# A decoder layer's MLP: additions of finished banks ahead of weight preparation, MLP buffers in other places, and a narrow first matmul in the second up unit

## The chip, the cores and the metric

The kernel runs on one core of a Trainium2 chip. The metric is the device time of one execution in microseconds (us). Five engines work beside each other, each on its own queue in order: TensorE (PE, with its weight loads PEld), VectorE (DVE), ScalarE (ACT), GpSimd (POOL) and SyncE (SP), which here issues nearly all DMA transfers. Matmuls accumulate in eight banks of PSUM; everything else lies in SBUF.

## The reference

One layer of a hybrid decoder: 256 tokens (T), model width 2048, MLP width 8192, all in float32.

```
h = rmsnorm(x, g_mix) @ w_in          # one projection for all head groups
y_ssd = ...                           # Mamba-2 heads, gated norm
y_att = ...                           # sparse attention with an indexer
x = x + concatenate([y_ssd, y_att]) @ w_out
u = rmsnorm(x, g_mlp) @ w_up
return x + square(relu(u)) @ w_down
```

The change touches the last two lines alone, the MLP.

## The kernel before, in words

**Precision.** TensorE multiplies in a reduced float32 type (fp32r). Every operand is therefore split into a rounded part "hi" and a remainder "lo", and a product is three matmuls: hi·hi, lo·hi and hi·lo (`three`, L199, L201, L202). The weights are split on the chip while they stream: `operands` issues the load (L151, tile `raw`, in the MLP `rawm`), ScalarE casts hi (L154) and VectorE forms lo = raw − hi (L155), both into one tile `w2`, in the MLP `w2m`. There are three `rawm` and three `w2m` buffers. This weight preparation runs under `tc.high_priority(offset=HP)`, HP = 600.

**Order.** TensorE's order is the order of the program. On the other engines a scheduler orders instructions by what they depend on and by priority; a higher offset puts an instruction earlier. Each engine then takes its queue strictly in the order written.

**Up.** The MLP width is worked in three parts h, of 10, 11 and 11 units of 256 columns (`PARTS`). `up(h)` computes a part: for each unit, `product_w` takes two weight tiles (c = 0, 1), with 16 steps each of a 512-column and a 256-column matmul (L240), 64 matmuls in all. ScalarE and VectorE make r from the banks (copy L847, add, square of relu) and split it into `uh` and `ul` (L862, L863). The very first unit is multiplied before the MLP's pools are open, with weights from the earlier pool `wts`.

**Down.** `down(h)` multiplies a part's units with the second weight matrix in two halves j of 1024 output columns. Each half goes over the part's units, here called pairs g. A pair is done in one of two ways. `plain` has 8 products (24 matmuls) from one `w2m`. `seven` has 7 products (21 matmuls) by a scheme of Strassen's kind; its weights are sums t of blocks (VectorE, L885 and L888; lo L891) in a `w2m`, and three blocks in a tile `wb` (L883, lo L890). Of `t` and `wb` there is one buffer each. A table `SEVEN` marks the pairs 1, 3, 5 and 7 (in two halves 9 too) as `seven`, so a half begins plain, seven, plain, seven.

**Banks.** The eight banks are four of tag "mid" and four of tag "acc". A half accumulates in four banks `outs` (`acc[b][c]`) of one tag; its seven-products use four more, `ps7`, of the other tag. So the first `seven` pair of the second half takes the four banks in which the first half accumulated. They come free when VectorE has done `add` (L910): xr += acc · rs4, 128x512 each, four of them. `ps7` is copied into a tile `m` (ScalarE, L937), combined by VectorE (L938, L939, L940) and added to xr by two additions of 1024 columns (also L910). In the last part the first half's four finished blocks of xr are then written out (L912).

**Memory.** `mid_stack.close()` gives the pools `wts` (57824 to 116448, in bytes of a partition) and `mid` (116448 to 213984) back before the MLP's pool opens. The MLP's tiles are then laid into the same addresses, and the first writer of a new tile waits for the last reader of the old ones there.

**Cutting.** `interrupted(kind)` tells whether something else was multiplied since the last product of that kind. If so, `product_w` splits its first matmul into 32 (FIRST_W) and 480 columns.

Of the kernel before, what the change touches and what calls it, by code (L numbers as in the profile page):

```python
# [9 lines left out]
F32 = mybir.dt.float32  # L10
F32R = mybir.dt.float32r
# [5 lines left out]
P = 128  # L17
D = 2048
T = 256
NB = T // P  # L20
# [7 lines left out]
HP = 600  # L28
# [3 lines left out]
WIDE_B = 3  # L32
# [3 lines left out]
SPARE = 64  # L36
# [11 lines left out]
PARTS = (0, 10, 21, 32)  # L48
# [5 lines left out]
E, G, P1, F, M6 = range(5)  # L54
# [34 lines left out]
def hymba_kernel(ctx: ExitStack, tc: tile.TileContext, xn, xt, w_in, w_out, w_up, w_down, vcol, vrow, out):  # L89
    nc = tc.nc  # L90
# [42 lines left out]
    mlp_pool = []  # L133

    def operands(src, n, load=None, shift=0, parts=2):

        pitch = (n + 63) // 64 * 64
        with tc.high_priority(offset=HP):
            if mlp_pool:
                raw = mlp_pool[0].tile([P, parts, pitch], F32, name="rawm", bufs=WIDE_R)  # L140
                both = mlp_pool[0].tile([P, 2 * parts * pitch + SPARE], F32R, name="w2m", bufs=WIDE_B)
            else:
                raw = wts.tile([P, parts, pitch], F32, name="raw", tag="raw", bufs=RB)
                both = wts.tile([P, 2 * parts * pitch + SPARE], F32R, name="w2", tag="w2", bufs=WB)
            hi, lo = (both[:, shift + i * parts * pitch:shift + (i + 1) * parts * pitch]
                      .rearrange("p (k c) -> p k c", k=parts)[:, :, :n] for i in range(2))
            src = src.rearrange("p (k c) -> p k c", k=parts)
            step = parts if load is None else 1
            for i in range(0, parts, step):
                s = slice(i, i + step)  # L150
                nc.sync.dma_start(raw[:, s, :n], src[:, s])  # L151
                if load is not None:
                    load()
                nc.scalar.copy(hi[:, s], raw[:, s, :n])  # L154
                nc.vector.tensor_tensor(lo[:, s], raw[:, s, :n], hi[:, s].bitcast(F32), op=OP.subtract)  # L155
        return hi, lo

    other = []
# [64 lines left out]
        other.append("narrow")  # L223
        return acc

    def product_w(src, right, tag="acc"):

        acc = [accumulator(tag), accumulator(tag)]
        n = KT if mlp_pool else 8
        for at in range(0, KT, n):  # L230
            for c, out in enumerate(acc):
                hi, lo = operands(src[c][:, at * P:(at + n) * P], P, shift=SHIFT_W, parts=n)
                for k in range(n):
                    x = right(at + k)
                    todo = [(hi, 0, 2 * T), (lo, 0, T)]

                    if interrupted("wide"):
                        todo[:1] = [(hi, 0, FIRST_W), (hi, FIRST_W, 2 * T - FIRST_W)]
                    for j, (w, fr, m) in enumerate(todo):
                        nc.tensor.matmul(walk(out[:, fr:fr + m]), w[:, k], walk(x[:, fr:fr + m]),  # L240
                                         start=(at + k + j == 0), stop=(at + k == KT - 1 and j == len(todo) - 1),
                                         skip_group_check=True)
                    if k % 4 == 3:
                        step()
        other.append("wide")
        return acc
# [50 lines left out]
    for name, cols in IN_BLOCKS:  # L297
        n = sum(b - a for a, b in cols)
# [440 lines left out]
    xr = []  # L739
# [72 lines left out]
    xr, box, ss2, squares = run()  # L812
# [6 lines left out]
    first = product_w(w_up[0], x2)  # L819
# [13 lines left out]
    mid_stack.close()  # L833


    mlp = ctx.enter_context(tc.tile_pool(name="mlp", bufs=1))
    mlp_pool.append(mlp)

    def up(h, tag):

        u = []
        for g in range(PARTS[h + 1] - PARTS[h]):
            n = (4, 8, 7)[sum(g in marked for marked in SEVEN[h])]
            full = mlp.tile([P, 8, P], F32, name="r")
            r = full[:, :4].rearrange("p (c b) t -> p c (b t)", c=2)
            for c, acc in enumerate(first if h + g == 0 else product_w(w_up[PARTS[h] + g], x2, tag)):
                nc.scalar.copy(r[:, c], acc[:, T:])  # L847
                nc.vector.tensor_tensor(r[:, c], r[:, c], acc[:, :T], op=OP.add)
            nc.vector.scalar_tensor_tensor(r, r, 0.0, r, op0=OP.max, op1=OP.mult)
            if n > 4:  # L850

                s3 = full[:, S3[n]]
                nc.vector.tensor_tensor(s3, full[:, A11], full[:, A21], op=OP.subtract)
                nc.vector.tensor_tensor(full[:, S2], full[:, A22], s3, op=OP.add)
                nc.vector.tensor_tensor(full[:, S1::2], full[:, A11:A22:2], full[:, S2, None].to_broadcast([P, 2, P]),
                                        op=OP.subtract)
            if h == 0 and g == 3:
                junk = mlp.tile([P, 5, 512], F32, name="m")
                row_factors([junk[:, b] for b in range(NB)])
            uh = mlp.tile([P, n, P], F32R, name="uh", tag=f"uh{g}", bufs=1)  # L860
            ul = mlp.tile([P, n, P], F32R, name="ul", tag=f"ul{g}", bufs=1)
            nc.scalar.copy(uh, full[:, :n])  # L862
            nc.vector.tensor_tensor(ul, full[:, :n], uh.bitcast(F32), op=OP.subtract)  # L863
            u.append((uh, ul))
        return u
# [7 lines left out]
    def seven(src):  # L873

        with tc.high_priority(offset=HP):
            raw = mlp.tile([P, 4, 512], F32, name="rawm", bufs=WIDE_R)
            nc.sync.dma_start(raw, src.rearrange("p (k c) -> p k c", k=4))
            t = mlp.tile([P, 4, 512], F32, name="t")
            wb = mlp.tile([P, 2 * 3 * 512 + SPARE], F32R, name="wb")
            wt = mlp.tile([P, 2 * 4 * 512 + SPARE], F32R, name="w2m", bufs=WIDE_B)  # L880
            (hb, lb), (ht, lt) = [[w[:, SHIFT + i * n * 512:SHIFT + (i + 1) * n * 512]
                                   .rearrange("p (k c) -> p k c", k=n) for i in range(2)] for w, n in ((wb, 3), (wt, 4))]
            nc.scalar.copy(hb, raw[:, 1:])  # L883

            nc.vector.tensor_tensor(t[:, :2], raw[:, 1::2], raw[:, :1].to_broadcast([P, 2, 512]), op=OP.add)  # L885
            nc.scalar.copy(ht[:, :2], t[:, :2])  # L886
            for i in range(2, 4):
                nc.vector.tensor_tensor(t[:, i], t[:, 2 * (i - 2)], raw[:, 5 - i], op=OP.add)  # L888
            nc.scalar.copy(ht[:, 2:], t[:, 2:])  # L889
            nc.vector.tensor_tensor(lb, raw[:, 1:], hb.bitcast(F32), op=OP.subtract)  # L890
            nc.vector.tensor_tensor(lt, t, ht.bitcast(F32), op=OP.subtract)  # L891
        return [(hb[:, i], lb[:, i]) for i in range(3)] + [(ht[:, i], lt[:, i]) for i in range(4)]

    def down(h, u, tags):
        pairs = len(u)
        for j in range(2):
            marked = SEVEN[h][j]
            end = h == 2 and j == 1
            outs = [accumulator(tags[j]) for _ in range(4)]
            acc = [outs[:2], outs[2:]]  # L900
# [7 lines left out]
            def add(b, c, src, store=False):  # L908
                c = slice(1024 * j + c.start, 1024 * j + c.stop)
                nc.vector.scalar_tensor_tensor(xr[:, b, c], src, rs4[:, b:b + 1], xr[:, b, c], op0=OP.mult, op1=OP.add)  # L910
                if store:
                    nc.sync.dma_start(out[b * P:(b + 1) * P, c], xr[:, b, c])  # L912

            half = [slice(0, 512), slice(512, 1024)]
            ps7 = None
            kept = []
            for g in range(pairs):
                w = (seven if g in marked else plain)(w_down[j, PARTS[h] + g])
                if g in marked:
# [12 lines left out]
                    go(acc[1][0], u[g], A22, t4, False)  # L932
                    if done:

                        m = mlp.tile([P, 5, 512], F32, name="m", bufs=1)
                        for i, p in ((P1, p1), (F, p5), (E, p7), (M6, p6)):
                            nc.scalar.copy(m[:, i], p)  # L937
                        nc.vector.tensor_tensor(m[:, M6], m[:, P1], m[:, M6], op=OP.subtract)  # L938
                        nc.vector.tensor_tensor(m[:, E], m[:, M6], m[:, E], op=OP.add)  # L939
                        nc.vector.tensor_tensor(m[:, G:F + 1:2], m[:, F, None].to_broadcast([P, 2, 512]), m[:, E::4],  # L940
                                                op=OP.subtract)
                        for b, i in ((0, P1), (1, E)):
                            add(b, slice(0, 1024), m[:, i:i + 2].rearrange("p k c -> p (k c)"))
                elif end and g >= pairs - 2:
                    kept.append((u[g], w))
                else:
# [2 lines left out]
                            for b in range(NB):  # L949
                                go(acc[b][c], u[g], 2 * k + b, w[k][c], g + k == 0, g == pairs - 1 and k == 1)  # L950
            if not end:
                for c in range(2):
                    for b in range(NB):
                        add(b, half[c], acc[b][c], h == 2)
                other.append("down")
                continue

# [5 lines left out]
            c = slice(0, 256)  # L963
# [4 lines left out]
            c = slice(256, 512)  # L968
# [75 lines left out]
```

## Time and profile before

| what | value |
|---|---|
| times of three runs | 1102.87, 1095.23, 1102.21 us; median 1102.21 |
| profiled execution | 1099.45 us |
| its span, first to last instruction | 1097.6 us |
| mean granted TensorE clock | 0.984 |
| TensorE busy | 1063.8 us, 97% |
| VectorE busy | 811.6 us, 74% |
| ScalarE busy | 560.0 us, 51% |
| DMA | 207.35 MB, mean 189 GB/s |
| first load of the MLP's own pool | 396.18 us |

The profile is of one execution. A row of the timeline gives the start, the busy time, the engine and line, the operation with out<-in, and in brackets how long the engine had been idle before and what ended that. A row of a window gives its length, the busy time of PE, PEld, DVE, ACT and POOL with the count of instructions, then the granted clock of TensorE (1.00 is full speed), the DMA engines' busy share and GB/s. Ends of matmuls are modelled: neighbouring rows overlap, and the distance from start to start tells the rate.

### The profile page before, as it was taken

Reading aid. Unit: us, or ns where it says so; the run is one execution under the profiler, and the core shown is the slowest. Engines: PE = TensorE matmul, PEld = TensorE weight load, DVE = VectorE, ACT = ScalarE, POOL = GpSimd, SP = SyncE. Lnnn points to the kernel's source line nnn. Section 1 sums busy time; section 2 is a strip of 40 time slices with the busy share of each in tenths; the row PEclk is TensorE's granted clock in tenths of the full one; section 3 lists DMA queues with packets and bytes.
Section 4 is the critical chain, followed back from the end, with each engine's and each line's share of the span. In section 5 each row is a group of like instructions: output and inputs, shape, how many; then the busy total and the mean of one; then the engine's idle time right before and its main releaser. Section 6 shows DMA issues by size and latency. Waiting matters only on the chain.

```text
span 1097.6 us, 14923 instructions
## 1 busy us (share of the span) xinstructions
PE 1063.8 (97%) x5937; PEld 938.4 (85%) x5937; DVE 811.6 (74%) x1014; ACT 560.0 (51%) x675; POOL 25.2 (2%) x30
## 2 busy tenths in 40 slices
PE   9999999999999969999979999999889999999798
PEld 7999999888888858888868888888778888888687
DVE  6777998687665555679886767699877666698965
ACT  7755455566654434455635344455535444455452
POOL 0020000121000000000000000000000000000000
PEclk9999999999999989999989999999989999999899
DMA  9865447543465445555645555546546555545552
GB/s 327 265 212 173 156 118 230 170 150 125 155 238 191 135 186 197 192 195 191 229 153 192 195 193 213 203 177 213 214 135 222 192 192 192 192 178 205 201 182 77
DMA packets 45461, 207.35 MB, mean 189 GB/s; under 512 B 5072, under 2 KB 9424, under 8 KB 29264
## 3 DMA queue, kind: packets, MB, share of 16 engines
q1 hardware_dynamic: 45248, 206.35, 54.2%
q8 instruction: 47, 0.77, 0.3%
q14 instruction: 22, 0.18, 0.0%
q10 hardware_dynamic: 144, 0.05, 0.0%
HBM read 204.29 MB, written 2.10 MB: 188 GB/s over the span
## 4 chain that ended last, share of the span: by engine, by line
PE 89%; DVE 7%; issue 1%; DMA 1%; ACT 1%; SPq 0%; DVEq 0%; ACTq 0%
PE acc L240 31%; PE acc L199 15%; PE acc L201 14%; PE acc L202 14%; PE acc L219 10%; DVE w2m L155 2%; DVE w2m L891 2%; DVE t L885 1%; DVE t L888 1%; DVE xr L910 1%; PE ps_y L620 1%; DVE wb L890 1%; DMA xT<-in_xt 0%; DMA rawm<-in_w_down 0%; PE ps_sr L704 0%
## 5 line engine op out<-in xcount | busy, mean ns | idle before, releaser
L240 PE MATMUL acc<-x2x,w2m 128*128 128x512 f32 (+2 forms) x1986 | 338.1, 331 | 8.4 <-ACT w2m L154 6.9
L240 PEld LDWEIGHTS acc<-x2x,w2m 128*128 128x128 f32 x1986 | 301.2, 189 | 45.2 <-ACT w2m L154 7.2
L155 DVE TENSOR_TENSOR w2m<-rawm,w2m 128x2048 fp32r<-128x2048 f32 x100 | 229.0, 2290 | 113.1 <-ACT w2m L154 113.0
L154 ACT CAST w2m<-rawm 128x2048 fp32r<-128x2048 f32 x100 | 190.3, 1903 | 168.0 <-PE acc L240 93.3
L155 DVE TENSOR_TENSOR w<-raw,w 128x1024 fp32r<-128x1024 f32 (+3 forms) x148 | 157.3, 1072 | 85.0 <-ACT w L154 84.8
L154 ACT CAST w<-raw 128x1024 fp32r<-128x1024 f32 (+3 forms) x148 | 133.7, 915 | 112.8 <-PE acc L202 58.3
L199 PE MATMUL acc<-w2m,uh 128*128 128x512 f32 (+4 forms) x424 | 158.5, 378 | 3.9 <-DVE xr L910 3.9
L201 PE MATMUL acc<-w2m,ul 128*128 128x512 f32 (+1 forms) x412 | 157.9, 383 | 0.0
L202 PE MATMUL acc<-w2m,uh 128*128 128x512 f32 (+1 forms) x412 | 157.5, 382 | 0.0
L219 PE MATMUL acc<-hx,w 128*128 128x256 f32 (+1 forms) x978 | 115.0, 277 | 0.0
L219 PEld LDWEIGHTS acc<-hx,w 128*128 128x128 f32 x978 | 112.7, 188 | 0.0
L199 PEld LDWEIGHTS acc<-w2m,uh 128*128 128x128 f32 x424 | 80.5, 190 | 18.6 <-issue 4.3
L201 PEld LDWEIGHTS acc<-w2m,ul 128*128 128x128 f32 x412 | 78.4, 190 | 13.4
L202 PEld LDWEIGHTS acc<-w2m,uh 128*128 128x128 f32 x412 | 78.3, 190 | 13.4
L199 PE MATMUL acc<-w,hx 128*128 128x512 f32 (+3 forms) x228 | 83.7, 370 | 0.5 <-ACT w L154 0.5
L201 PE MATMUL acc<-w,hx 128*128 128x512 f32 (+1 forms) x224 | 81.0, 361 | 0.0
L202 PE MATMUL acc<-w,hx 128*128 128x512 f32 (+1 forms) x224 | 80.8, 361 | 0.0
L891 DVE TENSOR_TENSOR w2m<-t,w2m 128x2048 fp32r<-128x2048 f32 x26 | 59.5, 2290 | 27.1 <-ACT w2m L889 25.6
L886 ACT CAST w2m<-t 128x1024 fp32r<-128x1024 f32 x26 | 27.3, 1049 | 75.8 <-PE acc L202 64.1
L199 PEld LDWEIGHTS acc<-w,hx 128*128 128x128 f32 x228 | 42.7, 188 | 6.9 <-ACT w L154 1.0
L883 ACT CAST wb<-rawm 128x1536 fp32r<-128x1536 f32 x26 | 38.4, 1475 | 19.1 <-PE acc L202 15.6
L890 DVE TENSOR_TENSOR wb<-rawm,wb 128x1536 fp32r<-128x1536 f32 x26 | 45.5, 1752 | 3.2 <-ACT wb L883 3.2
(235 smaller groups left out, 1172.4 us busy)
## 6 DMA issues: line engine op xcount, KB each, us to landing
rawm<-in_w_down SPq DMA_DIRECT2D x64, 1024.0 KB, 4.8
rawm<-in_w_up SPq DMA_DIRECT2D x62, 1024.0 KB, 4.8
raw<-in_w_in SPq DMA_DIRECT2D x72, 512.0 KB, 3.5
raw<-in_w_out SPq DMA_DIRECT2D x32, 512.0 KB, 3.3
raw<-in_w_in SPq DMA_DIRECT2D x16, 256.0 KB, 5.2
raw<-in_w_in SPq DMA_DIRECT2D x16, 152.0 KB, 5.2
raw<-in_w_in SPq DMA_DIRECT2D x8, 304.0 KB, 3.3
xT<-in_xt SPq DMA_DIRECT2D x8, 256.0 KB, 5.2
```

The costliest lines, as they stand in the source:

```text
L154: nc.scalar.copy(hi[:, s], raw[:, s, :n])
L155: nc.vector.tensor_tensor(lo[:, s], raw[:, s, :n], hi[:, s].bitcast(F32), op=OP.subtract)
L199: nc.tensor.matmul(go(out[:, i:j]), ah, go(wh[:, i:j]), start=first and i == 0, stop=False, skip_group_check=True)
L201: nc.tensor.matmul(go(out), al, go(wh), start=False, stop=False, skip_group_check=True)
L202: nc.tensor.matmul(go(out), ah, go(wl), start=False, stop=last, skip_group_check=True)
L219: nc.tensor.matmul(acc[:, c, at:at + n], w[:, 0, s], x[:, fr:fr + n], start=(i + k + j == 0), stop=(i >= 2 and k == 7 and j == len(todo) - ...
L240: nc.tensor.matmul(walk(out[:, fr:fr + m]), w[:, k], walk(x[:, fr:fr + m]), start=(at + k + j == 0), stop=(at + k == KT - 1 and j == len(t ...
L620: nc.tensor.matmul(pt[:, 64 * i:64 * i + 64], m[i // 4][:, i % 4, :], xdt[:, c, 64 * h:64 * h + 64], start=True, stop=True)
L883: nc.scalar.copy(hb, raw[:, 1:])
L886: nc.scalar.copy(ht[:, :2], t[:, :2])
L890: nc.vector.tensor_tensor(lb, raw[:, 1:], hb.bitcast(F32), op=OP.subtract)
L891: nc.vector.tensor_tensor(lt, t, ht.bitcast(F32), op=OP.subtract)
```

## The change

Three things are changed.

1. At the end of a half, the four additions of its finished banks get the priority 2·HP, above weight preparation. The two additions of m, which came ahead of them in the program, come behind them in a function `combine` with no priority of its own. In the last part the first half's output is written in two DMAs of 1024 columns, after `combine`, instead of four of 512.
2. A new pool `units`, opened before `mlp`, holds `uh`, `ul`, `m`, `t` and `wb`. In `mlp` stay `r`, `w2m` and `rawm`, with `w2m` allocated ahead of `rawm`. Sizes and buffer counts are the same. Before, `rawm` lay at 66016 to 90592 and `w2m` at 90592 to 140512, in the place of `wts`. Now `units` lies at 57824 to 150240, `r` at 150240, the `w2m` buffers at 154336, 170976 and 187616, and the `rawm` buffers at 204256, 212448 and 220640, in the place of `mid` and behind it.
3. `product_w` of the second unit (h = 0, g = 1) always splits its first matmul into 32 and 480 columns.

```
@@ operands
             if mlp_pool:
+                both = mlp_pool[0].tile([P, 2 * parts * pitch + SPARE], F32R, name="w2m", bufs=WIDE_B)
                 raw = mlp_pool[0].tile([P, parts, pitch], F32, name="rawm", bufs=WIDE_R)
-                both = mlp_pool[0].tile([P, 2 * parts * pitch + SPARE], F32R, name="w2m", bufs=WIDE_B)
@@ product_w
-    def product_w(src, right, tag="acc"):
+    def product_w(src, right, tag="acc", again=False):
...
+        if again:
+            other.append("again")
@@ behind mid_stack.close()
+    units = ctx.enter_context(tc.tile_pool(name="units", bufs=1))
     mlp = ctx.enter_context(tc.tile_pool(name="mlp", bufs=1))
@@ up
-            for c, acc in enumerate(first if h + g == 0 else product_w(w_up[PARTS[h] + g], x2, tag)):
+            for c, acc in enumerate(first if h + g == 0 else product_w(w_up[PARTS[h] + g], x2, tag, h == 0 and g == 1)):
...
-            uh = mlp.tile([P, n, P], F32R, name="uh", tag=f"uh{g}", bufs=1)
-            ul = mlp.tile([P, n, P], F32R, name="ul", tag=f"ul{g}", bufs=1)
+            uh = units.tile([P, n, P], F32R, name="uh", tag=f"uh{g}", bufs=1)
+            ul = units.tile([P, n, P], F32R, name="ul", tag=f"ul{g}", bufs=1)
@@ seven
-            t = mlp.tile([P, 4, 512], F32, name="t")
-            wb = mlp.tile([P, 2 * 3 * 512 + SPARE], F32R, name="wb")
+            t = units.tile([P, 4, 512], F32, name="t")
+            wb = units.tile([P, 2 * 3 * 512 + SPARE], F32R, name="wb")
@@ down
+            def combine(m):
+                for b, i in ((0, P1), (1, E)):
+                    add(b, slice(0, 1024), m[:, i:i + 2].rearrange("p k c -> p (k c)"))
...
-                        m = mlp.tile([P, 5, 512], F32, name="m", bufs=1)
+                        m = units.tile([P, 5, 512], F32, name="m")
...
-                        for b, i in ((0, P1), (1, E)):
-                            add(b, slice(0, 1024), m[:, i:i + 2].rearrange("p k c -> p (k c)"))
+                        if end:
+                            combine(m)
...
             if not end:
-                for c in range(2):
+                with tc.high_priority(offset=2 * HP):
+                    for c in range(2):
+                        for b in range(NB):
+                            add(b, half[c], acc[b][c])
+                combine(m)
+                if h == 2:
                     for b in range(NB):
-                        add(b, half[c], acc[b][c], h == 2)
+                        nc.sync.dma_start(out[b * P:(b + 1) * P, 1024 * j:1024 * j + 1024],
+                                          xr[:, b, 1024 * j:1024 * j + 1024])
```

Lines behind the touched places move by two to seven: L240 is now L242, L847 is L850, L862 is L865, L877 is L880, L885 is L888, L888 is L891, L890 is L893, L891 is L894, L910 is L913, L912 is L915, L938 to L940 are L945 to L947.

VectorE's queue in the middle part (h = 1), where the first half ends and the second begins. Numbers tell one tile from another: m_6891 is the first half's m, w2m_6971 and t_6969 belong to the second half's first seven pair (g = 1), w2m_7006 to the plain pair g = 2, t_7036 and w2m_7038 to the seven pair g = 3, acc_6563 is the first half's first bank. Before:

```order
L939 TENSOR_TENSOR m_6891<-m_6891 128x512
L891 TENSOR_TENSOR w2m_6971<-t_6969,w2m_6971 128x2048
L940 TENSOR_TENSOR m_6891<-m_6891 128x2x512
L885 TENSOR_TENSOR t_7036<-rawm_7034 128x1024
L155 TENSOR_TENSOR w2m_7006<-rawm_7005,w2m_7006 128x2048
L888 TENSOR_TENSOR t_7036<-t_7036,rawm_7034 128x512
L910 SCALAR_TENSOR_TENSOR xr_3345<-m_6891,rs4_4108,xr_3345 128x1024
L888 TENSOR_TENSOR t_7036<-t_7036,rawm_7034 128x512
L910 SCALAR_TENSOR_TENSOR xr_3345<-m_6891,rs4_4108,xr_3345 128x1024
L891 TENSOR_TENSOR w2m_7038<-t_7036,w2m_7038 128x2048
L910 SCALAR_TENSOR_TENSOR xr_3345<-acc_6563,rs4_4108,xr_3345 128x512
```

After (the same tiles have numbers a few higher: m_6895, the banks acc_6567 to acc_6570, w2m_6975, w2m_7009, t_7040):

```order
L946 TENSOR_TENSOR m_6895<-m_6895 128x512
L913 SCALAR_TENSOR_TENSOR xr_3345<-acc_6567,rs4_4108,xr_3345 128x512
L913 SCALAR_TENSOR_TENSOR xr_3345<-acc_6569,rs4_4108,xr_3345 128x512
L913 SCALAR_TENSOR_TENSOR xr_3345<-acc_6568,rs4_4108,xr_3345 128x512
L913 SCALAR_TENSOR_TENSOR xr_3345<-acc_6570,rs4_4108,xr_3345 128x512
L894 TENSOR_TENSOR w2m_6975<-t_6973,w2m_6975 128x2048
L155 TENSOR_TENSOR w2m_7009<-rawm_7010,w2m_7009 128x2048
L888 TENSOR_TENSOR t_7040<-rawm_7038 128x1024
L947 TENSOR_TENSOR m_6895<-m_6895 128x2x512
L891 TENSOR_TENSOR t_7040<-t_7040,rawm_7038 128x512
```

All four additions of banks now stand directly behind the second combination of m, ahead of the remainders of the pairs g = 1 and g = 2; before, the first of them stood behind the remainder of g = 3. The combination's last step (L947) and the two additions of m have moved behind weight preparation.

ScalarE's queue at the MLP's start, from the last cast of the weights of the first up unit on. x2x is the normalized input of the up product, r the result of an up unit, w2m a weight tile of the MLP. Before:

```order
L154 CAST w_4086<-raw 128x1024
L708 ACTIVATE x2x<-ps_sr,vc 128x256 x4
L847 COPY r<-acc 128x256 x2
L791 ACTIVATE m,ss_3350<-xr 128x512 x2
L862 CAST uh<-r 128x512
L154 CAST w2m<-rawm 128x2048 x4
L847 COPY r<-acc 128x256
```

After:

```order
L154 CAST w_4086<-raw 128x1024
L710 ACTIVATE x2x<-ps_sr,vc 128x256 x4
L154 CAST w2m<-rawm 128x2048 x2
L850 COPY r<-acc 128x256
L154 CAST w2m<-rawm 128x2048
L850 COPY r<-acc 128x256
L793 ACTIVATE m,ss_3350<-xr 128x512 x2
L865 CAST uh<-r 128x512
```

The first two casts of MLP weights now stand ahead of the copies of the first unit's result, and the third between the two copies. On SyncE, the first load into the MLP's pool waited for the last matmul of the first up unit, for VectorE and for several earlier loads; it now waits for the last matmul of the output projection (384.27 us in the profile before) and for GpSimd alone.

More of the change, by code (lines that the diff above doesn't have):

```diff
@@ L857, in up @@
             if h == 0 and g == 3:
-                junk = mlp.tile([P, 5, 512], F32, name="m")
+                junk = units.tile([P, 5, 512], F32, name="m")
                 row_factors([junk[:, b] for b in range(NB)])
-            uh = mlp.tile([P, n, P], F32R, name="uh", tag=f"uh{g}", bufs=1)
-            ul = mlp.tile([P, n, P], F32R, name="ul", tag=f"ul{g}", bufs=1)
+            uh = units.tile([P, n, P], F32R, name="uh", tag=f"uh{g}", bufs=1)
+            ul = units.tile([P, n, P], F32R, name="ul", tag=f"ul{g}", bufs=1)
             nc.scalar.copy(uh, full[:, :n])
```

## The prediction

> **What bounds the kernel now.** I read the page's engine totals first, then its chain, the list of what TensorE waited for, TensorE's timeline at the longest of those waits, and the windows behind them.
>
> ```profile
> PE 1063.8 (97%) x5937; PEld 938.4 (85%) x5937; DVE 811.6 (74%) x1014; ACT 560.0 (51%) x675; POOL 25.2 (2%) x30
> POOL 0020000121000000000000000000000000000000
> PEclk9999999999999989999989999999989999999899
> PE 89%; DVE 7%; issue 1%; DMA 1%; ACT 1%; SPq 0%; DVEq 0%; ACTq 0%
> ```
>
> TensorE is the bound: busy for 97% of the 1097.6 us, 89% of the chain that ended last. Other work can give back only what makes TensorE stand still or run at less than its rate. The PEclk line dips in four slices. The waits, as total, times, longest:
>
> ```profile
> PE acc L199 <- DVE xr L910: 19.8, 4, 6.8
> PE acc L240 <- ACT w2m L154: 6.9, 1, 6.9
> PE acc L240 <- DVE w2m L155: 1.5, 1, 1.5
> ```
>
> 28.2 us of idle TensorE, in two kinds of place. TensorE's timeline (start, length, line, in brackets the idle time before) shows where:
>
> ```profile
> 402.98 0.80 PE L240 MATMUL acc<-x2x,w2m 128*128 128x512 f32 x1 [6.87 <-ACT w2m L154]
> 562.35 0.46 PE L199 MATMUL acc<-wb,uh 128*128 128x512 f32 x1 [2.30 <-DVE xr L910]
> 569.93 0.77 PE L199 MATMUL acc<-w2m,uh 128*128 128x512 f32 x1 [3.94 <-DVE xr L910]
> 798.96 0.76 PE L199 MATMUL acc<-wb,uh 128*128 128x512 f32 x1 [6.78 <-DVE xr L910]
> 1040.26 0.77 PE L199 MATMUL acc<-wb,uh 128*128 128x512 f32 x1 [6.78 <-DVE xr L910]
> ```
>
> The first is at the MLP's second up unit. The others stand where a part's second half meets its first seven-product pair: the fresh banks for it are those of the half before, and VectorE has not added them to xr. Windows behind the waits (length, busy times, then the granted clock):
>
> ```profile
> 405.30:411.20 5.90, 5.89 (x18) 5.06 (x19) 4.59 (x2) 2.03 (x2) 0.00 (x0) 0.50 0.86 308
> 562.30:565.80 3.50, 3.45 (x15) 2.73 (x15) 3.50 (x4) 2.18 (x2) 0.00 (x0) 1.00 0.63 260
> 569.90:575.10 5.20, 5.17 (x12) 4.13 (x13) 1.44 (x3) 1.90 (x1) 0.00 (x0) 0.50 0.42 176
> 798.90:803.80 4.90, 4.84 (x12) 3.81 (x13) 4.22 (x6) 0.59 (x1) 0.00 (x0) 0.50 0.00 0
> 1040.20:1046.10 5.90, 5.84 (x14) 4.61 (x15) 4.30 (x7) 1.47 (x1) 0.00 (x0) 0.50 0.46 178
> ```
>
> Behind the 2.30 us wait the clock stays 1.00; behind the four places with 3.94 us or more it is 0.50 for 5.89 + 5.17 + 4.84 + 5.84 = 21.7 us. Half of that, 10.9 us, is lost as well. The Trainium skill, "TensorE: Matmul & The Clock Gate", Part 1, says that the clock halves after about 3.4 us without work and returns after about 3.4 us of work; the trace agrees, with 2.30 harmless, 3.94 halving, and returns after about 5 to 6 us.
>
> **The change part by part.**
>
> *MLP start.* The first three rows are the chain of work, the fourth and fifth ScalarE's timeline, the last the window before the stall.
>
> ```profile
> 384.27 2.85 PE acc L240 x17
> 387.99 8.13 PE acc L240 x49
> 396.18 4.83 DMA rawm<-in_w_up
> 387.59 1.94 ACT L708 ACTIVATE x2x<-ps_sr,vc 128x256 fp32r<-128x256 f32 x4 [4.88 <-PE ps_sr L704]
> 403.52 1.90 ACT L154 CAST w2m<-rawm 128x2048 fp32r<-128x2048 f32 x1 [0.59 <-DMA rawm<-in_w_up]
> 384.20:396.00 11.80, 11.80 (x75) 10.53 (x73) 2.80 (x6) 1.82 (x4) 0.00 (x0) 1.00 0.00 0
> ```
>
> The load of the second unit starts at 396.18, when the first unit's last matmul (387.99 + 8.13) is done, because its target lies in the memory that this unit's weights occupy; for 11.8 us ahead of it the DMA engines are idle (share 0.00). In the new places it waits only for the output projection's last matmul, done at 384.27, and for GpSimd, whose line shows no work after the tenth slice. New chain: load 384.3 to 389.1 (4.83); ScalarE has its x2x rows until 389.5 (387.59 + 1.94), casts until 391.4 (1.90); VectorE's remainder takes 2.29 (row below), until 393.7. The second load lands 2.5 us after the first (casts at 403.52 and one 2.49 earlier, as the stall ending at 402.98 shows with 1.90 of cast before it), cast by 393.5, remainder by 396.0. TensorE wants the first at 396.1, the second 16 x (0.22 + 0.11) = 5.3 us later. Spare 2.4 and 5.4 us: the 8.4 us of idle and 2.9 of half clock go. What is next late is nothing here; the third load is wanted a unit (10.7 us, below) later.
>
> *Additions first.* VectorE and TensorE at h=1:
>
> ```profile
> 784.98 0.69 DVE L939 TENSOR_TENSOR m<-m 128x512 f32<-128x512 f32 x1
> 785.59 2.29 DVE L891 TENSOR_TENSOR w2m<-t,w2m 128x2048 fp32r<-128x2048 f32 x1
> 787.79 1.22 DVE L940 TENSOR_TENSOR m<-m 128x1024 f32<-128x1024 f32 x1
> 788.93 1.22 DVE L885 TENSOR_TENSOR t<-rawm 128x1024 f32<-128x1024 f32 x1
> 792.26 0.68 DVE L888 TENSOR_TENSOR t<-t,rawm 128x512 f32<-128x512 f32 x1
> 792.87 1.28 DVE L910 SCALAR_TENSOR_TENSOR xr<-m,rs,xr 128x1024 f32<-128x1024 f32 x1
> 798.06 0.75 DVE L910 SCALAR_TENSOR_TENSOR xr<-acc,rs,xr 128x512 f32<-128x512 f32 x1
> 851.34 2.72 DVE L910 SCALAR_TENSOR_TENSOR xr<-acc,rs,xr 128x512 f32<-128x512 f32 x4
> 786.73 0.38 PE L199 MATMUL acc<-w2m,uh 128*128 128x512 f32 x1
> 791.79 0.39 PE L202 MATMUL acc<-w2m,uh 128*128 128x512 f32 x1
> ```
>
> The half's first matmul is at 786.73, its 24th, the last before the stall, at 791.79: 23 steps of 0.22 us, so the next is due at 792.0. The first add comes at 798.06, behind ten instructions of weight preparation and combination. In the new order the four adds come right behind L939 (now L946): 785.59 to 788.3 (2.72 for four in a row). Their banks are finished in time: the last four groups of half 0 have three matmuls of 0.22 each, so bank 1 gets its last matmul ten before 786.73, at 784.5, ends at 784.9, and the others follow by 0.66; each add starts about 0.7 us after its bank is done. So the banks are free at 788.3, 3.7 us before they are wanted.
>
> What is queued behind the adds on VectorE is weight preparation, 2.7 us later than before:
>
> ```profile
> L155 DVE TENSOR_TENSOR w2m<-rawm,w2m 128x2048 fp32r<-128x2048 f32 x100 | 229.0, 2290 | 113.1 <-ACT w2m L154 113.0
> L890 DVE TENSOR_TENSOR wb<-rawm,wb 128x1536 fp32r<-128x1536 f32 x26 | 45.5, 1752 | 3.2 <-ACT wb L883 3.2
> ```
>
> L891 now ends at about 788.3 + 2.2 = 790.5; TensorE wants it at the tenth matmul group's third product, 792.0 + 11 x 0.22 = 794.4. L155 of pair 2 ends at 792.7, wanted behind 21 matmuls and one more, 792.0 + 22 x 0.22 = 796.8. Then pair 3's sums with the rest of m and its first addition between them, 1.22 + 1.22 + 0.68 + 1.28 + 0.68, and wb, 1.75: 6.8 us, to 799.5; wb's remainder is wanted 47 matmuls after 792.0, at 802.3. Spare is 3 to 4 us everywhere. It does not shrink: a plain and a seven pair want 24 + 21 matmuls of 0.22 = 9.9 us from TensorE and 2.29 + 1.22 + 2 x 0.68 + 1.75 + 2.29 = 8.9 us from VectorE (L155, L885, L888, L890, L891). All 19.8 us of idle and the other 7.9 us of half clock go.
>
> The adds of the second half stand at the same place as before (851.34, behind the last product); one m addition of 1.28 us moves ahead of a remainder there, hidden by up matmuls. In the last part two output writes of twice the size replace four, and wait for the m additions, with SyncE's next loads behind them:
>
> ```profile
> 1040.14 4.64 SPq L912 DMA_DIRECT2D out_y<-xr  x4
> 1047.81 0.34 SPq L151 DMA_DIRECT2D rawm<-in_w_down  x1
> ```
>
> The next load was issued 3.0 us after the last of four writes, so it waited for its own buffer, not for them. I cost the writes at nothing; if this cover is gone, one wait like the 2.30 us above.
>
> Had VectorE reached an add before its bank was done, every remainder behind it would be late by that wait, and what exceeds the 3 us of spare would come back as idle TensorE; by the rows above that wait is nothing. A rule that speaks against such an order stands in the same page of the Trainium skill, section "Architectural detail: the array is 16× 32×32, not 1× 128×128": VectorE's queue is strictly first in, first out. By that rule nothing behind the add could pass it; the trace leaves 0.7 us, so the sum is the same by both, and the rule bears on the late VectorE below.
>
> *Rate of the long products.* Up units of h=1 and h=2 from the chain, both at clock 1.00:
>
> ```profile
> 614.34 117.45 PE acc L240 x705
> 852.53 120.57 PE acc L240 x705
> ```
>
> The same 705 matmuls take 3.1 us more in h=2. Nothing waits in either; the difference is a rate that begins behind the h=1 stall. I take it that without this stall h=2 keeps the rate of h=1: 3.1 us gained, and 0.8 for the 47 us between stall and up, chosen between nothing and 47 x 3.1/117.5 = 1.2. Bounds for both together: nothing and 4.3.
>
> *32 columns first.* One matmul more and the same columns: at most an average matmul, 117.45/705 = 0.17; I take 0.1. Should it set units 2 to 10 to the slower rate, 9 x 3.1/11 = 2.6; a gain is excluded only by these units already going at the fast rate of h=1.
>
> *Buffer places.* Same sizes and counts: nothing, except for a rival below.
>
> **Sum.** 28.2 + 10.9 + 3.1 + 0.8 - 0.1 = 42.9 us. The profiled run took 1099.45 us (span and 1.85 around it), 2.8 under the median of 1102.21: 1099.45 - 42.9 = 1056.5 us. Idle times are counted from a matmul's modelled end, 0.38 after its start, though the next starts after 0.22, so each of five stalls hides about 0.16 more, and the restarts (0.76 to 0.80 for the first matmul) some: up to 2 us below, 1054.5.
>
> **Rivals.**
>
> *VectorE becomes late.* For it: 8.9 of 9.9 us, and 2.7 us of adds plus 3.8 of m work (1.22 + 2 x 1.28) fall into the first cycle. Against it: 3 to 4 us of spare. If the waits only shrink to what h=0 shows, 2.30 or 3.94 + 2.6 us at each of three transitions, 7 to 20 us come back: 1063 to 1076.
>
> *The slow rate is kept.* For it: I know its start, not its cause. h=2 only: 1060.4; also units 2 to 10: 1063; also every up unit of h=1: 1066.
>
> *The first load is still held,* so the change does not do this part: 8.4 + 2.9 = 11.3 back, 1068. Against it: idle DMA and only two waits left on that load.
>
> *Slower:* the new places make TensorE's reads of w2m and wb slower. From 402.98 to the end of the span are 694.6 us; without the waits in it (19.8 + 1.5) and the 10.9 of half clock, TensorE works for 662. So 42.9 us are used up at 6.5%, a spacing of 0.2343 instead of 0.22; at 0.24 (9.1%) the time is 1056.5 + 60 = 1117. Against it: the three w2m buffers rotate within 117.45 us without one standing out.
>
> **How the numbers follow.** Forecast 0.63 (1052 to 1059), slow rate 0.17, late VectorE 0.13, held load 0.05, slower 0.02. The range from 1051 (the finer count, and run to run) to 1068 leaves out most of the late VectorE and the slower case, about 0.13. A measurement of this kernel can tell about 1% from no change: under 1091 faster 0.96, within 0.02, slower 0.02.
>
> **What would show it.** The waits on additions and on the first cast gone from TensorE's list; no clock of 0.50 after 10 us; additions of acc ending about 4 us before the first seven pair of each second half; the first MLP load near 384; h=2's up near 117.5; TensorE's chain share above 95%. I am wrong if TensorE waits for L155, L893 or L894 behind the transitions, or if the L242 rate rises in h=0.

## The result, and the profile after

The changed kernel takes 1054.19 us (median of four runs, 1053.49 to 1054.87), before 1102.46; the ratio is 0.958, with a 95% interval of 0.954 to 0.962. The forecast was 1056.5, range 1051 to 1068. The profiled execution took 1053.77 us, its span 1052.0. The kernel before spreads from 1092.9 to 1106.9 us over all the comparisons below, the changed kernel over 1.4 us; each comparison has runs of its own of the kernel before.

The engine totals, the clock and the chain of the page after:

```profile
PE 1047.2 (100%) x5938; PEld 930.5 (88%) x5938; DVE 810.9 (77%) x1014; ACT 558.5 (53%) x675; POOL 25.2 (2%) x30
PEclk9999999999999999999999999999999999999999
PE 100%; DVE 0%; POOL 0%; issue 0%; POOLq 0%
```

TensorE is busy for the whole span, the four dips of its clock are gone, and the chain that ended last is TensorE alone. VectorE does the same work (810.9 against 811.6 us) in less time. All that is left in the list of TensorE's waits is one at the kernel's very start:

```profile
PE ps_w L257 <- POOL ones L252: 1.3, 1, 1.3
```

The MLP's start, from the timelines of SyncE, ScalarE and VectorE:

```profile
383.81 14.40 SPq L151 DMA_DIRECT2D rawm<-in_w_up  x6
388.89 1.90 ACT L154 CAST w2m<-rawm 128x2048 fp32r<-128x2048 f32 x1
391.02 1.91 ACT L154 CAST w2m<-rawm 128x2048 fp32r<-128x2048 f32 x1 [0.23 <-DMA rawm<-in_w_up]
390.83 4.50 DVE L155 TENSOR_TENSOR w2m<-rawm,w2m 128x2048 fp32r<-128x2048 f32 x2 [1.31 <-ACT w2m L154]
```

and the piece of the chain there:

```profile
387.46 104.25 PE acc L242 x626
```

The first load is issued at 383.81 instead of 396.18. The casts follow at 388.89 and 391.02, both remainders are done at 395.3, and up matmuls run from 387.46 without a break through all ten units. The first tile of the second unit is ready near 393.1, and TensorE comes to it at 395.4; the second, ready at 395.3, is wanted some 5 us later.

The transition of h = 1, on VectorE and TensorE:

```profile
763.10 0.69 DVE L946 TENSOR_TENSOR m<-m 128x512 f32<-128x512 f32 x1
763.71 2.72 DVE L913 SCALAR_TENSOR_TENSOR xr<-acc,rs,xr 128x512 f32<-128x512 f32 x4
766.34 2.28 DVE L894 TENSOR_TENSOR w2m<-t,w2m 128x2048 fp32r<-128x2048 f32 x1
768.54 2.29 DVE L155 TENSOR_TENSOR w2m<-rawm,w2m 128x2048 fp32r<-128x2048 f32 x1
775.42 1.75 DVE L893 TENSOR_TENSOR wb<-rawm,wb 128x1536 fp32r<-128x1536 f32 x1
777.08 2.29 DVE L894 TENSOR_TENSOR w2m<-t,w2m 128x2048 fp32r<-128x2048 f32 x1
769.99 0.38 PE L199 MATMUL acc<-wb,uh 128*128 128x512 f32 x1
780.33 0.38 PE L202 MATMUL acc<-wb,uh 128*128 128x512 f32 x1
782.31 0.38 PE L202 MATMUL acc<-w2m,uh 128*128 128x512 f32 x1
```

The additions are over at 766.4, and TensorE takes the first of these banks at 769.99: 3.6 us of spare, and as much in h = 2. In h = 0 the scheduler left L947 and L894 ahead of the additions; they end at 545.1, the bank is taken at 547.3, and the spare is 2.2 us. Pair 3's wb is done at 777.2 and its remainder is read at 780.33 (3.2 us); its w2m is done at 779.4 and read at 782.31 (2.9 us, the least here).

Stage by stage, from the first matmul of a stage to that of the next, worked out from the starts in the two traces (up h=0 is counted from its 18th matmul, behind a few transposes; the last stage ends with the start of its last matmul):

```
                     up h=0   down 0   up h=1   down 1   up h=2   down 2
before (us)          116.38   110.05   117.45   120.73   120.57   120.59
after (us)           104.34   100.62   117.45   110.53   117.45   110.60
difference            12.04     9.43     0.00    10.20     3.12     9.99
```

That is 44.8 us of the 45.7 between the two profiled executions; 0.5 more lies ahead of the MLP, where the change alters nothing: the MLP begins at 383.73 instead of 384.27.

### The profile page after: what moved, and what is told of

The parts are those of the page before. It is cut to its first block, busy times and chain, and to the rows that moved or that the text cites. A ratio compares the mean times of both kernels' runs of the same rounds, so it can differ in the third digit from the quotient of the medians.

```text
span 1052.0 us, 14902 instructions
## 1 busy us (share of the span) xinstructions
PE 1047.2 (100%) x5938; PEld 930.5 (88%) x5938; DVE 810.9 (77%) x1014; ACT 558.5 (53%) x675; POOL 25.2 (2%) x30
## 4 chain that ended last, share of the span: by engine, by line
PE 100%; DVE 0%; POOL 0%; issue 0%; POOLq 0%
PE acc L242 33%; PE acc L199 17%; PE acc L202 17%; PE acc L201 17%; PE acc L219 11%; PE ps_y L622 1%; PE ps_sr L706 0%; PE ps_l L660 0%; PE ps_o L685 0%; PE ps_w L257 0%; PE ps_s L512 0%; PE ps_s L513 0%; PE ps_dec L613 0%; PE ps_pt L677 0%; PE ps_yo L628 0%; PE pt_q L378 0%
## 5 line engine op out<-in xcount | busy, mean ns | idle before, releaser
L242 PE MATMUL acc<-x2x,w2m 128*128 128x256 f32 (+2 forms) x1987 | 331.5, 327 | 0.0
L242 PEld LDWEIGHTS acc<-x2x,w2m 128*128 128x128 f32 x1987 | 298.0, 188 | 33.3
L199 PE MATMUL acc<-w2m,uh 128*128 128x512 f32 (+4 forms) x424 | 156.3, 373 | 0.0
L199 PEld LDWEIGHTS acc<-w2m,uh 128*128 128x128 f32 x424 | 79.4, 188 | 13.4
L894 DVE TENSOR_TENSOR w2m<-t,w2m 128x2048 fp32r<-128x2048 f32 x26 | 59.5, 2288 | 11.9 <-ACT w2m L892 11.0
L893 DVE TENSOR_TENSOR wb<-rawm,wb 128x1536 fp32r<-128x1536 f32 x26 | 45.6, 1753 | 4.5 <-ACT wb L886 4.4
L865 ACT CAST uh<-r 128x512 fp32r<-128x512 f32 (+2 forms) x32 | 24.5, 766 | 44.8 <-DVE r L852 42.7
```

What stands on the lines that cost most here:

```text
L199: nc.tensor.matmul(go(out[:, i:j]), ah, go(wh[:, i:j]), start=first and i == 0, stop=False, skip_group_check=True)
```

## The experiments

**Each part alone.** First the additions alone:

```
-    units = ctx.enter_context(tc.tile_pool(name="units", bufs=1))
     mlp = ctx.enter_context(tc.tile_pool(name="mlp", bufs=1))
+    units = mlp                     # all tiles of the MLP in one pool, rawm ahead of w2m
...
-  product_w(w_up[PARTS[h] + g], x2, tag, h == 0 and g == 1)
+  product_w(w_up[PARTS[h] + g], x2, tag)
```

> Additions first, with the MLP's buffers in their old places and no forced 32-column cut in the second up unit. Theory (the parts are independent): the stall at the second up unit stays (6.9 + 1.5 us idle, then a clock of 0.50 for about 6 us), the four waits on additions go. From the starts of matmuls in the profile before, the three transitions lose 9.4, 9.5 and 10.0 us with their half-clock stretches, and the slower rate 3.9: 32.8 us, so 1099.5 - 32.8 = 1067 us. Rival (the parts help each other): additions first pay only when the weights come earlier, and 1075 us or more remain.

Measured: 1065.45 us (1064.52 to 1067.62), ratio 0.971 (0.968 to 0.974). TensorE's waits:

```profile
PE acc L242 <- ACT w2m L154: 6.9, 1, 6.9
PE acc L242 <- DVE w2m L155: 1.5, 1, 1.5
```

and the two rows of its timeline behind them:

```profile
402.71 0.79 PE L242 MATMUL acc<-x2x,w2m 128*128 128x512 f32 x1 [6.86 <-ACT w2m L154]
405.04 100.42 PE L242 MATMUL acc<-x2x,w2m 128*128 128x256 f32 x575 [1.53 <-DVE w2m L155]
```

No addition is waited for any more, and the second unit's stall is there as before: the first theory, near its 1067. This part needs nothing of the others.

Then the places alone; the hunks in `down` are undone, and there is no forced cut:

```
-                        if end:
-                            combine(m)
+                        combine(m)
...
-                with tc.high_priority(offset=2 * HP):
-                    for c in range(2): ...        # add(b, half[c], acc[b][c]); combine(m); out
+                for c in range(2):
+                    for b in range(NB):
+                        add(b, half[c], acc[b][c], h == 2)
```

> New buffer places alone: additions in their old order and with their old priority, no forced cut. Theory: the first load of the MLP is issued near 384, the stall at the second up unit (12.2 us with its half clock) goes, and 19.8 us of waits on additions with three stretches at a clock of 0.50 stay: 1099.5 - 12.2 = 1087 us. The up product of the last part stays at 120.6 us, since the stalls set its rate. Rival (the places set the rate): that product takes 117.5 us, and the time is 1083 to 1084 us.

Measured: 1085.88 us (1082.91 to 1094.70, seven runs), ratio 0.990 (0.987 to 0.993). The profiled execution is the slowest of them, 1094.70. TensorE's wait, then the up products of h = 1 and h = 2 in the chain:

```profile
PE acc L199 <- DVE xr L913: 19.1, 4, 6.9
```

```profile
605.07 120.57 PE acc L242 x705
846.45 120.57 PE acc L242 x705
```

The stall at the second unit is gone and the waits on additions are not. Both later up products go at the slower rate in this execution, so the places alone do not prevent it; the other six runs have no profile. Against 1098.1 in its own comparison the median is 12.2 us lower, the price of that stall as expected, though the seven runs lie up to 11.8 us apart. The new pool and the exchange of `w2m` and `rawm` were not tried apart.

**Without the cut.**

```
-  product_w(w_up[PARTS[h] + g], x2, tag, h == 0 and g == 1)
+  product_w(w_up[PARTS[h] + g], x2, tag)
```

> The change without the 32-column cut in the second up unit. Theory: the cut costs and brings nothing that can be measured: within 0.5 us of the changed kernel, 1053.5 to 1054.9 us. Rival: without the cut units 2 to 10 go at the slower rate of 3.1 us per 11 units, 2.6 us more: 1056.5 us.

Measured: 1054.17 us (1053.25 to 1054.87), the changed kernel's own time. Up units of h = 0 in the chain:

```profile
387.99 104.12 PE acc L242 x625
```

One matmul less and 0.13 us less than 104.25, at the same rate. The cut costs what it was taken for, 0.1, and brings nothing while there is no stall ahead of it. Additions alone, with the cut kept, ask whether it helps behind one (the edit is that of additions alone, without its last two lines):

> Additions first and the 32-column cut, with the MLP's buffers in their old places. Theory: the stall at the second up unit stays, and the cut neither shortens it nor sets the rate behind it: as with additions first alone, 1064 to 1068 us. Rival (the cut is there to restore the rate after a stall): up units 3 to 10 go at the fast rate in each run, and all times lie at the lower end, 1064 us or below.

Measured: 1065.53 us (1064.38 to 1071.19) beside 1065.45 without it, so no gain in the median. The profiled execution, the fastest of its runs, did go at the fast rate behind the stall:

```profile
404.45 97.89 PE L242 MATMUL acc<-x2x,w2m 128*128 128x256 f32 x575 [1.35 <-DVE w2m L155]
```

Here 575 matmuls take 97.89 us, with additions alone 100.42, with about equal stretches at half clock. But the kernel before, which has no such cut, went at the fast rate there too (98.98 us for these matmuls, 6.1 us of them at half clock against 3.9 here), and the cut did not bring the times to the lower end. The rival falls as it was put; a weaker effect stays open.

**Which half of the additions' edit does it.** Program order alone, without the priority:

```
-                with tc.high_priority(offset=2 * HP):
-                    for c in range(2):
-                        for b in range(NB):
-                            add(b, half[c], acc[b][c])
+                for c in range(2):
+                    for b in range(NB):
+                        add(b, half[c], acc[b][c])
                 combine(m)
```

> The change, but the four additions come ahead of those of m in the program only, without the higher priority. Theory (both are needed, since weight preparation has a priority of its own): VectorE's queue holds the first addition behind L894, L947, L888, L155 and L891 in h = 1 and h = 2, so from the changed kernel's profile it ends 1.7 us after its bank is wanted, and the fourth addition, behind L894, L893 and L888 more, about 5 us after: 6.7 us of waits and 2.6 of half clock in each of these two, none in h = 0 (there the four come early enough): 1053.8 + 18.6 = 1072 us, up to 1077 with the slower rate behind the waits. Rival (the place in the program is enough): no waits, 1054 us.

Measured: 1073.00 us (1070.01 to 1075.33). VectorE, and the waits of TensorE at h = 1:

```profile
763.46 2.28 DVE L894 TENSOR_TENSOR w2m<-t,w2m 128x2048 fp32r<-128x2048 f32 x1
770.74 0.74 DVE L913 SCALAR_TENSOR_TENSOR xr<-acc,rs,xr 128x512 f32<-128x512 f32 x1
778.33 0.74 DVE L913 SCALAR_TENSOR_TENSOR xr<-acc,rs,xr 128x512 f32<-128x512 f32 x1
771.63 0.47 PE L199 MATMUL acc<-wb,uh 128*128 128x512 f32 x1 [1.58 <-DVE xr L913]
779.21 0.46 PE L199 MATMUL acc<-w2m,uh 128*128 128x512 f32 x1 [3.97 <-DVE xr L913]
```

Between L946 and the first addition stand five instructions of preparation and combination, as expected, and the fourth addition comes 7.6 us after the first. h = 0 has no wait. Now the priority alone:

```
-                        if end:
-                            combine(m)
+                        combine(m)
...
                             add(b, half[c], acc[b][c])
-                combine(m)
```

> The change, but the four additions have the higher priority only, and stand behind those of m in the program. Theory: they add to the same elements of xr, so they cannot pass the m additions, which have no priority. In h = 1 and h = 2 the first then comes 3.5 us late and the last another 3 to 4, 7 us of waits and 2.6 to 5 of half clock each; in h = 0 the last comes 2 us late: 1053.8 + 22 = 1076 us, up to 1083 with the slower rate. Rival (priority is enough): 1054 us.

Measured: 1077.50, 1080.51 and 1083.13 us, and one run of 2327.45 that no profile explains (the median is 1081.82 with it, 1080.51 without); ratio 0.983 (0.977 to 0.988), without that run.

```profile
PE acc L199 <- DVE xr L913: 15.1, 5, 3.4
```

Five waits, one in h = 0 (2.08 us) and two in each later part. The additions cannot pass those of m, which change the same elements of xr. So both halves of the edit are needed: the order in the program lets the additions go first, the priority makes them.

**VectorE's spare.** Additional work behind the four additions:

```
                             add(b, half[c], acc[b][c])
+                    for i in range((4, 7, 10)[h] if j == 0 else 0):
+                        piece = xr[:, 1, 1024 * j:1024 * j + 1024]
+                        nc.vector.tensor_tensor(piece, piece, piece, op=OP.max)
                 combine(m)
```

> The change, with additional VectorE work of 1.13 us each (xr = max(xr, xr) over 128x1024, which changes no value) behind the four additions at the end of the first half: 4 pieces in part h = 0, 7 in h = 1, 10 in h = 2, among the weight preparation. Theory (VectorE has 3 to 4 us of spare, and the 2.3 us of m work move behind): 4 pieces, 4.5 us, cost nothing; 7 pieces, 7.9 us, cost 7.9 - 2.3 - 3 = 2.6 us of waits and leave the clock at 1.00 if none is over about 3 us; 10 pieces, 11.3 us, cost about 6 us of waits, and half a clock stretch of 2.6 us more if a single wait is 3.9 us or longer. In all 1062 to 1066 us. Rival (VectorE is already the bound there): every piece costs its own time, 21 x 1.13 = 23.7 us: 1077 us.

Measured: 1071.08 us (one run). TensorE's waits:

```profile
PE acc L202 <- DVE w2m L894: 6.6, 6, 2.0
PE acc L202 <- DVE wb L893: 1.7, 1, 1.7
PE acc L202 <- DVE w2m L155: 0.8, 2, 0.4
```

The up products of h = 1 and h = 2 in its chain:

```profile
594.54 120.57 PE acc L242 x705
831.11 117.45 PE acc L242 x705
```

23.7 us of work cost 9.1 us of waits: 0.75 in h = 0, where none was expected, 3.7 in h = 1 (2.6 expected) and 4.6 in h = 2 (6 expected; it came in four waits, none over 1.7 us). The rival's 1077 is not reached, so VectorE is not the bound, and the spare is real. But the time is above the 1062 to 1066 us expected, and 17.3 us above the changed kernel's profiled run, not 9.1. The MLP began 0.8 us later, the up product of h = 1, behind a wait of 0.75 us, took 3.1 us more, and the three down stages lost 13.4 us: the listed waits, the slower rate behind some of them, the part of each wait that the modelled ends hide, and gaps too short to be listed. A short wait can cost more than its length.

**What sets the rate.** The change without cuts in `down`:

```
-CUTS = {0: 320, 5: 144, 8: 160, 13: 160, 16: 160}
+CUTS = {}
```

> The change with no cuts of matmuls at the start of a down half (the table CUTS left empty; 15 matmuls fewer). Theory (the slower rate comes from stalls alone, and there are none): the down stages keep their 100.6, 110.5 and 110.6 us, 1053 to 1055 us in all. Rival (the cuts restore the rate at each change from up to down, whatever came before): some 1480 matmuls of down go at 0.2233 instead of 0.2200 us, 4.9 us more: 1059 us.

Measured: 1067.61 us (1067.22 to 1068.30). Two things changed. One is a wait of 4.6 us in h = 0:

```profile
505.43 0.77 PE L199 MATMUL acc<-w2m,uh 128*128 128x512 f32 x1 [4.62 <-DVE r L851]
```

VectorE's queue came out in another order there (an L851 behind L894, L893 and L888); why fewer matmuls make it so was not tried. The other is the rate. It is the slower one already ahead of that wait, twelve matmuls of the first down stage in 2.68 us, 0.2233 each:

```profile
497.31 0.39 PE L199 MATMUL acc<-wb,uh 128*128 128x512 f32 x1
499.99 0.39 PE L199 MATMUL acc<-w2m,uh 128*128 128x512 f32 x1
```

Later on it is the same. The up product of h = 2 and, from row to row, nine matmuls of the last down stage, in the chain of this kernel:

```profile
829.59 120.57 PE acc L242 x705
...
990.15 0.22 PE acc L202
...
992.16 0.22 PE acc L202
```

and the same in the changed kernel:

```profile
820.32 117.45 PE acc L242 x705
...
990.00 0.22 PE acc L202
...
991.98 0.22 PE acc L202
```

2.01 us for nine against 1.98: 0.2233 and 0.2200 us each. There is no wait at all between 510 us and the end of this kernel, and from there on all down stages go at 0.2233, and h = 2's up product takes 120.57 us. So my theory that only stalls set the slower rate fell. What stands: the cuts at a down stage's start (five matmuls of its first half) bring the fast rate, and a rate, once set, can last for hundreds of matmuls. Of the 13.7 us between the profiled executions, 7.5 lie in the first down stage with its wait, 2.8 in the other two, and 3.1 in the up product of h = 2.

This pointed to the products of 512 columns ahead of the MLP, where many matmuls go at 0.2233. Two versions with more cuts there, beside the changed kernel again:

```
# more cuts: after every interruption          # spaced cuts: every fourth step
+ cut = interrupted("product") and n == 512    + 320 if n == 512 and kt % 4 == 0 and b == 0 else None
  (inside the loop over kt, used at b == 0)
```

> The change, and in the products with 512 columns ahead of the MLP a first matmul of 320 + 192 columns after every interruption by other matmuls, not only at a block's start (24 matmuls more). Theory (cuts restore the rate there as in down): of about 890 matmuls of 512 columns some 450 go at 0.2233 instead of 0.2200 us, 1.5 us; a cut costs 475 - 440 = 35 ns, 0.8 in all: 0.7 us less than the changed kernel at best, 1053.5 us. Rival (the slower rate there comes back at once, as it does a few matmuls after the cuts that are there now): 0.8 us more, 1055 us.

> The change, and in the same products a cut of 320 + 192 columns at every fourth step, four to a block instead of one (28 matmuls more). Theory (repeated cuts hold the rate): up to 1.5 us less for 1.0 us of cuts, 1053.7 us. Rival (the rate does not hold): 1 us more, 1055.2 us.

> The changed kernel itself, as the measure for the two others of this series: 1053.5 to 1054.9 us, TensorE at the rate of 0.2200 us in every down stage and 117.45 us for the up products of h = 1 and h = 2.

Measured: 1055.16 us (1054.66 to 1056.11), 1056.59 (1055.59 to 1057.52), and 1054.42 (1053.87 to 1054.89) for the changed kernel, within 0.25 us of its first median. The MLP's stages are the same in all three to 0.03 us; in the profiled executions the MLP only begins 2.3 us later in both versions. By the medians the cuts cost 0.7 and 2.2 us, and the rate does not hold between the interruptions: with cuts after every interruption some 560 of the 512-column matmuls ahead of the MLP went at the slower rate, in the eleven executions with neither kind of cut 385 to 461. That is both rivals, and the spaced cuts cost more than theirs. No version here beats the changed kernel.

## Why the prediction was right, point by point

- **The bound.** TensorE was the bound and is now the whole chain. Right.
- **MLP start.** Taken at 8.4 + 2.9 = 11.3 us, measured 12.04. First load, casts and remainders came within 0.7 us of the times worked out. The places alone show that this part is theirs.
- **Additions.** Taken at 19.8 + 7.9 = 27.7 us; measured 9.43 + 10.20 + 9.99 = 29.6, of which about 0.7 in h = 1 is rate. Spare at the banks in h = 1: 3.7 forecast, 3.6 found; but "3 to 4 us everywhere" was read from h = 1 alone, and in h = 0 it is 2.2. The output writes, taken at nothing, show no wait in h = 2. Nine instructions, not ten, stood between L939 and the first addition before. Both halves of the edit were shown to be needed.
- **Modelled ends.** The stated correction of up to 2 us was real, and I should have taken it into the sum: the waits and half-clock stretches together brought 41 us, not 39.1. Some of it is the ends, some the half clock outside the windows that I counted: behind the first wait the trace has 0.50 up to 411.45 us and from before TensorE resumed at 402.98, where my window ran from 405.30 to 411.20.
- **Rate.** 3.1 + 0.8 taken, 3.12 and about 0.7 found. The size was right and the reason half so: a stall can set the slower rate, but so can a change of product without cuts. Up products of h = 1 and h = 2 with a wait in the down stage ahead were slow in 4 of 10 profiled cases; of 15 with no wait ahead and with the cuts none was. The rate at the end of the down stage ahead divides the 26 cases better: behind 0.2200 none of 18 was slow, behind 0.2233 five of 8. This chance may be a large part of the spread of before; no run shows that.
- **The cut.** 0.1 taken, 0.13 found. (9 x 3.1/11, given as 2.6, is 2.5, which is also what 100.42 and 97.89 us differ by.)
- **Rivals.** Late VectorE did not come; it needs several us of additional work in a cycle, and then costs more than its waits. The held load and slower places did not come. The slow rate did not come, and the version without cuts in `down` shows that these cuts, not the absence of stalls alone, prevent it in the down stages.
- **Place of the error.** Between the profiled executions 45.7 us went, 42.9 were forecast. Of the 2.8 us, 1.9 are the waits and half-clock stretches counted too short, 0.5 lies ahead of the MLP, where a wait of 0.5 us of the execution before did not return (chance, since the change does not reach there), and the rest outside the stages.

## What to carry to other kernels

An engine that is nearly always busy still hides what its waits cost: add to each wait the stretch at half clock that may follow it, and the rate at which it starts again. Where additions free accumulators for the next product, put them ahead of weight preparation in both ways, in the order of the program and in priority, after making sure from the trace that the banks are finished when the queue reaches them. Memory that a later phase loads into belongs where the readers ahead finish first, or the load waits for them.

## What the runs showed of the hardware that I had not expected

The clock can halve after the work has begun again, and behind waits that are shorter than one that left it alone. Places alone, the first wait of h = 0, in TensorE's timeline:

```profile
551.11 0.46 PE L199 MATMUL acc<-wb,uh 128*128 128x512 f32 x1 [2.09 <-DVE xr L913]
```

and the windows behind it:

```profile
551.10:552.00 0.90, 0.89 (x4) 0.79 (x5) 0.90 (x2) 0.40 (x1) 0.00 (x0) 1.00 0.77 255
552.00:555.40 3.40, 3.40 (x10) 2.67 (x9) 3.08 (x3) 1.55 (x2) 0.00 (x0) 0.51 0.53 222
```

A wait of 2.09 us, 0.9 us of work at full clock, then 3.4 us at half. Priority alone has the same behind 2.08 us in h = 0, and behind 2.78 in h = 2, there 1.3 us late:

```profile
1028.15 0.48 PE L199 MATMUL acc<-w2m,uh 128*128 128x512 f32 x1 [2.78 <-DVE xr L913]
```

```profile
1028.10:1029.40 1.30, 1.25 (x5) 0.97 (x6) 1.30 (x2) 0.00 (x0) 0.00 (x0) 1.00 0.68 120
1029.40:1032.80 3.40, 3.40 (x10) 2.60 (x9) 1.86 (x3) 1.48 (x1) 0.00 (x0) 0.52 0.95 313
```

The wait of 2.30 us in the kernel before was followed by 3.5 us at 1.00. So the reading in the prediction, 2.30 harmless and 3.94 halving, was no threshold for the length of a wait. The changes of the clock that the traces hold show what counts instead. In each trace they lie whole multiples of 3.413 us apart (before, the half clock begins at 401.21, 568.46, 797.15 and 1036.09 us, 49, 116 and 186 such steps after the first), and a stretch at half clock that ends before the kernel does lasts one, two or three steps: 3.41, 6.83 or 10.24 us, often partly within the wait. So the clock changes only at the borders of windows of 3.413 us, and what decides is how much of a wait falls into one window. For the waits of 2.30 and 3.94 us before:

```profile
558.22:561.63 3.41, 1.83 (x9) 1.22 (x7) 3.41 (x4) 1.04 (x1) 0.00 (x0) 1.00 0.00 0
561.63:565.05 3.42, 2.70 (x12) 2.27 (x13) 3.42 (x5) 1.43 (x2) 0.00 (x0) 1.00 0.93 302
565.05:568.46 3.41, 0.94 (x5) 0.46 (x3) 3.41 (x3) 1.10 (x1) 0.00 (x0) 1.00 0.01 5
```

The border at 561.63 splits the 2.30 us into 1.58 and 0.72, and the clock stays; the third window has 2.47 us without work, and behind it come 6.83 us at half. Over the MLP in all 13 traces, the clock halves behind every full-clock window with 2.06 us or more of idle TensorE (18 of them) and behind none with 1.96 or less, idle time being counted from the modelled ends. The limit between them, about 2 us of a window, is an estimate from these counts. Where a border falls against a wait is not fixed, so equal waits cost differently: the two of 6.78 us before were followed by 4.84 and 5.84 us at half. The Trainium skill, "TensorE: Matmul & The Clock Gate", Part 1, has a free-running window of about 3.4 us, and these traces agree with it; that the clock halves only after at least one such window without work does not agree with 2.06 us of idle in one.

And equal matmuls have two rates, 0.2200 and 0.2233 us for 512 columns (117.45 and 120.57 us for 11 up units), which can hold for hundreds of matmuls; no run shows why there are two.
